# Bias bands from the host, and dense tiles dealt over the jobs of attention and the samples' compressed branch

## The chip, the cores and the metric

One core of one Trainium2 chip. The metric is the device time of one execution in microseconds. Float32 data throughout; large matmuls take fp32r operands split into a high and a low part.

## The reference, cut to what matters

One layer of a hybrid decoder for a prompt of 512 rows and 8 samples of one row each with 1024 cached rows. h = x(1 + scale) + shift goes through one wide input projection. Two mixers run on its parts: native sparse attention (8 heads on 2 groups of keys: a compressed, a selected and a window branch, gated) and MoBA (8 heads, blocks of 256). Every logit gets a T5 bias by distance. Then gates, two up projections, a merge by sigmoid gates, an output projection, a residual and a layer norm.

```python
parts = jnp.split(h @ w_in, np.cumsum(IN_WIDTHS)[:-1], axis=-1)
(a_q, a_kc, a_vc, a_ks, a_vs, a_kw, a_vw, a_g, a_z, b_q, b_k, b_v, b_z, m_a, m_b) = parts
# each branch: softmax(q . k / 8 + bias[bucket(distance)]) v
y_a = (o_a * silu(a_z)) @ w_up_a
y_b = (o_b * silu(b_z)) @ w_up_b
mixed = (sigmoid(m_a) * y_a + sigmoid(m_b) * y_b) @ w_out
x_new = layer_norm(ALPHA * x + gate * mixed, ln_g, ln_b)
```

For the prompt all blocks are selected, so both mixers are causal attention there. The samples read their caches (cmp, slc, moba: 64 pages of 128 rows) and select blocks.

## The kernel before, in words

**Dense tiles.** The input projection is cut into tiles of 128 output channels, named in FILLS: q, z, bq, bz, bk, bv, vs, vw, kw, and m0 to m7, each of which is two tiles, ma and mb. `dense` makes a tile with 48 matmuls (8 steps of depth, 3 products of high and low parts, 2 halves of 260 columns) in 4 units of 12. Its weights come through the feed W: one load of 512 KB on SP's queue into a ring of 4 raw tiles, a copy on ACT (L310) and a subtraction on POOL or DVE (L231) into the split hl. W follows one fixed list, SEQ. K and V tiles are also written out (`evac`, ok); m tiles made while attention runs go to DRAM and back (m_d).

**Order.** The program is written by generators that `merge` interleaves: of several flows the one that has done the smallest share of its total goes next. Totals are written by hand (PHIS, ATT, DEC, and 5328 for a dense tile). A scheduler then fixes the order on each engine when the kernel is compiled: by its own estimate of times it issues the ready instruction that stands first in the program. `issue_after` and `order` add an edge of issue order on one engine, without a wait for completion; `high_priority` puts an instruction ahead of the rest of the program. On the chip each engine and SP's queue run strictly in that order.

**Stages.** (1) Start: adaLN, the tiles kc, vc, ks, and the bias tables (`tables`). (2) FILLS[0] merged with `phis`, which compresses the cached rows of the samples. At its end POOL's queue sends the band bs (16 heads x 384 biases, repeated for 128 rows) into the DRAM tile band_d, L939. (3) `dec_cmp`: the compressed branch of the samples, written into the program alone (drain, L942). (4) Attention of the prompt, `attend` for 8 pairs of heads: pairs 0 to 3 with 4 jobs, pairs 4 to 7 with 2. `prepare` loads the pair's band from band_d by a shifted view (L960) and splits q. A job scores 4 row tiles (`score`: 2 matmuls into one of 2 PSUM banks s, a minimum with the band on DVE at L1011, exp on ACT at L1015, scaling on POOL at L1017), turns p with 10 transposes (L1024), and every second job `value` multiplies by V; the pipe is three jobs deep. Each pair is merged with FILLS[pi + 1] and with a part of `dec`, up to DEC_SHARE[pi] of DEC. (5) `dec` is the samples' attention over the feed C: loads of 1 MB into 2 buffers, of which slck takes 16 issues on SP each, mobk and mobv 4, and slcv two gathers on POOL's queue. (6) FILLS[9] merged with the rest of `dec`. (7) up and output projections and the norm.

SP's queue issues the weight loads, the cache loads, the bands and the stores, one behind the other.

## Time and profile before

| | us |
|---|---|
| Median of 3 runs | 657.74 (655.98 to 663.47) |
| Profiled execution, its own time | 656.24 |
| Span of its trace, first to last instruction | 654.5 |
| TensorE (PE) busy | 610.4 |
| VectorE (DVE) busy | 311.0 |
| ScalarE (ACT) busy | 294.9 |
| GpSimd (POOL) busy | 288.5 |
| Mean granted TensorE clock, share of full speed | 0.984 |

Times in the trace count from the span's start. Attention's exps run from 184.7 to 489.3; the up projections begin at 541. TensorE's matmuls are pipelined, so a busy TensorE is not one at its peak.

### The profile page before, as it was taken

Reading aid. Unit: us, or ns where it says so; the run is one execution under the profiler, and the core shown is the slowest. Engines: PE = TensorE matmul, PEld = TensorE weight load, DVE = VectorE, ACT = ScalarE, POOL = GpSimd, SP = SyncE. Lnnn points to the kernel's source line nnn. Section 1 sums busy time; section 2 is a strip of 40 time slices with the busy share of each in tenths; the row PEclk is TensorE's granted clock in tenths of the full one; section 3 lists DMA queues with packets and bytes.
Section 4 is the critical chain, followed back from the end, with each engine's and each line's share of the span. In section 5 each row is a group of like instructions: output and inputs, shape, how many; then the busy total and the mean of one; then the engine's idle time right before and its main releaser. Section 6 shows DMA issues by size and latency. Waiting matters only on the chain.

```text
span 654.5 us, 13320 instructions
## 1 busy us (share of the span) xinstructions
PE 610.4 (93%) x4747; PEld 509.7 (78%) x4747; DVE 311.0 (48%) x800; ACT 294.9 (45%) x679; POOL 288.5 (44%) x328
## 2 busy tenths in 40 slices
PE   5999999999979699999999899998987999999993
PEld 4779999999968378776879679866635998999672
DVE  1465545433563663334355447735431155545177
ACT  2247556434444445534445447635333353432521
POOL 1105586551442323433364545535332264655646
PEclk9999999999999979999999999999999999999997
DMA  8995565539943683798875562269887353345202
GB/s 305 355 292 187 169 193 171 170 76 109 200 140 103 203 334 109 251 312 290 262 252 157 209 226 91 62 224 325 295 265 280 97 166 126 97 130 180 78 28 104
DMA packets 64132, 124.77 MB, mean 191 GB/s; under 512 B 8142, under 2 KB 28368, under 8 KB 63521
## 3 DMA queue, kind: packets, MB, share of 16 engines
q1 hardware_dynamic: 61954, 116.58, 53.6%
q0 software_dynamic: 2112, 7.34, 6.3%
q8 instruction: 37, 0.61, 0.4%
q14 instruction: 29, 0.24, 0.1%
HBM read 112.76 MB, written 11.13 MB: 189 GB/s over the span
## 4 chain that ended last, share of the span: by engine, by line
PE 57%; DMA 12%; SPq 5%; DVE 3%; issue 2%; POOL 1%; ACT 1%; POOLq 0%; ACTq 0%; DVEq 0%
PE d L199 33%; PE s L199 8%; PE e L199 6%; DMA band_d<-bs 6%; SPq L721 4%; DMA raw<-mobv 4%; PE pt L1024 3%; PE o L202 2%; PE o L199 2%; PE pt L199 1%; PE e L202 1%; DMA ew<-tabx 1%; DMA raw<-slcv,vidx 1%; DMA raw<-winv 1%; SPq L717 1%
## 5 line engine op out<-in xcount | busy, mean ns | idle before, releaser
L199 PE MATMUL d<-hTh,hl 128*128 128x260 f32 (+1 forms) x1408 | 269.4, 288 | 1.6 <-DVE hl L231 1.1
L199 PEld LDWEIGHTS d<-hTh,hl 128*128 128x128 f32 (+1 forms) x1408 | 218.6, 187 | 15.8 <-issue 9.4
L199 PE MATMUL d<-hTl,hl 128*128 128x260 f32 (+1 forms) x704 | 199.5, 284 | 0.0
L199 PEld LDWEIGHTS d<-hTl,hl 128*128 128x128 f32 (+1 forms) x704 | 131.6, 187 | 3.1 <-issue 2.5
L231 POOL TENSOR_TENSOR hl<-raw,hl 128x512 fp32r<-128x512 f32 x56 | 74.0, 1321 | 101.6 <-ACT hl L310 97.0
L310 ACT CAST hl<-raw 128x512 fp32r<-128x512 f32 (+1 forms) x111 | 67.8, 615 | 75.5 <-PE d L199 63.0
L1017 POOL TENSOR_SCALAR p<-p,sm,gp 128x512 f32<-128x512 f32 (+1 forms) x64 | 39.9, 623 | 95.9 <-DVE sm L1016 91.3
L1015 ACT ACTIVATE p<-s,sm 128x512 f32<-128x512 f32 (+1 forms) x96 | 50.8, 529 | 66.9 <-PE pt L1024 52.2
L231 DVE TENSOR_TENSOR hl<-raw,hl 128x512 fp32r<-128x512 f32 (+1 forms) x55 | 53.5, 974 | 49.1 <-ACT hl L310 47.3
L199 PE MATMUL d<-yh,hl 128*128 128x260 f32 x256 | 46.3, 282 | 0.0
L1024 PE MATMUL pt<-cst,p 128*128 128x128 f32 x240 | 40.6, 283 | 1.5 <-DVE pp L1029 0.8
L199 PEld LDWEIGHTS d<-yh,hl 128*128 128x128 f32 x256 | 39.8, 188 | 1.0 <-issue 0.4
L199 PE MATMUL s<-kd,q 128*128 128x512 f32 (+1 forms) x96 | 35.2, 367 | 4.6 <-ACT p L1015 4.6
L1009 DVE TENSOR_REDUCE sm<-s 128x1 f32<-128x256 f32 (+1 forms) x48 | 16.9, 354 | 42.7 <-PE s L199 41.7
L1024 PEld LDWEIGHTS pt<-cst,p 128*128 128x128 f32 x240 | 28.0, 143 | 11.6 <-issue 5.9
L199 PE MATMUL d<-yl,hl 128*128 128x260 f32 x128 | 36.0, 282 | 0.0
L1017 POOL TENSOR_SCALAR p<-p,sm,cst 128x512 f32<-128x512 f32 (+3 forms) x32 | 19.5, 608 | 37.2 <-DVE sm L1016 36.8
L1011 DVE CUSTOM_DVE_ANT_0 s<-s,band 128x256 f32<-128x256 f32 (+1 forms) x48 | 17.3, 362 | 36.8 <-PE s L199 23.6
L199 PEld LDWEIGHTS s<-kd,q 128*128 128x128 f32 x96 | 18.4, 191 | 18.3 <-ACT p L1015 7.7
L199 PE MATMUL s<-u,w1h 128*128 128x256 f32 (+1 forms) x160 | 30.1, 283 | 2.1 <-ACT u L827 0.8
L199 PE MATMUL s<-kd,qx 128*128 128x512 f32 (+1 forms) x96 | 31.5, 331 | 0.0
L231 POOL TENSOR_TENSOR u<-craw,u 128x512 fp32r<-128x512 f32 x16 | 22.0, 1377 | 21.6 <-ACT u L827 21.6
(425 smaller groups left out, 1158.3 us busy)
## 6 DMA issues: line engine op xcount, KB each, us to landing
raw<-w_cols SPq DMA_DIRECT2D x46, 512.0 KB
raw<-mobk SPq DMA_DIRECT2D x64, 256.0 KB
raw<-mobv SPq DMA_DIRECT2D x64, 256.0 KB
u<-ada_ss SPq DMA_DIRECT2D x16, 512.0 KB
craw<-cmp SPq DMA_DIRECT2D x64, 128.0 KB
raw<-slck SPq DMA_DIRECT2D x64, 64.0 KB
raw<-ada_g SPq DMA_DIRECT2D x8, 512.0 KB
raw<-w_up SPq DMA_DIRECT2D x8, 512.0 KB
```

What stands on the lines that cost most here:

```text
L199: i = mmraw(out, lhsT, rhs, start=start, stop=stop, skip_group_check=True)
L202: i = mmraw(out, lhsT, rhs, start=start, stop=stop, skip_group_check=True)
L231: (nc.gpsimd if eng == "p" else nc.vector).tensor_sub(out, x, f32(hi))
L310: nc.scalar.copy(h, src)
L717: _, pages = nc.values_load_multi_w_load_instructions(ptt[0:1, k0:k0 + step * (len(outs) - 1) + 1:step], engines=(mybir.EngineType.SP,), m ...
L721: dyn.append(nc.sync.dma_start(out, A[name][bass.ds(page, 1)].rearrange("a p c -> p (a c)")))
L1009: nc.vector.tensor_reduce(sm[:, 0:1], s[:, :b], axis=AX, op=OP.min)
L1011: nc.vector.tensor_tensor_reduce(out=s[:, b:n], in0=s[:, b:n], in1=j.band[:, 256 - (n - b):], scale=1.0, scalar=top, op0=OP.add, op1=OP.mi ...
L1015: nc.scalar.activation(pr, s[:, :n], AF.Exp, scale=-1.0, bias=sm[:, 1:2], accum_out=sm[:, 2:3])
L1017: nc.gpsimd.tensor_scalar(pr, pr, sm[:, 3:4], j.gate(i), op0=OP.mult, op1=OP.mult)
L1024: nc.tensor.transpose(p[:, k * 128:k * 128 + 128], j.p[i][:, kb * 128:kb * 128 + 128], ident)
```

## The change

The bias bands are computed on the host, one [128, 2, 256] tile for each pair (input `band`); the device keeps the last bias of each head in every partition (blast) and turns the loaded band into blast - band with two POOL instructions. band_d, bs, its matmul, its copy and its write are gone. The tiles bq2, bq0 and bq3 are merged with `dec_cmp` (CMP_FILLS); the other lists are dealt anew, ATT and DEC_SHARE too. The first matmul of every unit of a dense tile stands in issue order behind the 12th last score of the program (`hold`); the matmuls of `dec_cmp` stand behind the dense matmul written last (`behind`). From attention on, weight loads and the stores of ok and m_d have high priority (W.first).

```diff
+FILLS = [["ks", "vs", "ag", "vw", "q0", "kw", "q1", "q2", "q3"],
+         ["bq1", "m0", "m1"],
+         ["bv0", "bk0", "m2"],
+         ["z0", "bv1", "m3"],
+         ["z1", "bv2", "m4"],
+         ["bk1", "z2"],
+         ["bk2", "bv3", "bk3"],
+         ["z3", "bz0"],
+         ["bz1", "m5"],
+         ["bz2", "m6", "g0", "g1", "bz3", "g2", "g3", "m7"]]
+CMP_FILLS = ["bq2", "bq0", "bq3"]
-DEC_SHARE = [0.09, 0.15, 0.28, 0.31, 0.37, 0.45, 0.52, 0.66]
+DEC_SHARE = [0.13, 0.26, 0.39, 0.5, 0.57, 0.64, 0.78, 0.92]
-ATT = [20400, 20000, 17000, 47040, 10800, 5250, 7500, 9000]
+ATT = [17100] * 4 + [7100] * 3 + [11000]
+AHEAD = 12
-BAND_AT = 3
...
+    scored, dense_mm = [], []
+
+    def hold(i):
+
+        if len(scored) >= AHEAD:
+            order(i, scored[-AHEAD])
+
+    def behind(i):
+
+        order(i, dense_mm[-1])
+        return i
...
-                    if self.after is None:
+                    if self.first:
+                        with tc.high_priority():
+                            fn(t[:, :n])
+                    elif self.after is None:
...
-            p = p_e()
-            mm(p[:16, :384], tabx[:, 0:16], e[:, E_BAND:E_CMP], True, True)
-            bs = st.tile([16, 384], F32, name="bs")
-            nc.vector.tensor_copy(bs, p[:16, :384])
-            D["band"] = bs
...
+            nc.sync.dma_start(blast, bass.AP(tensor=A["tabx"].tensor, offset=A["tabx"].offset + 31 * 272, ap=[[0, 128], [1, 16]]))
...
-                            mm(acc[bk][:M, :HB], hl[:, x, kk * M:kk * M + M], hb[:, k, bk * HB:bk * HB + HB],
-                               k == 0 and j == 0, k == 7 and j == 2)
+                            i = mm(acc[bk][:M, :HB], hl[:, x, kk * M:kk * M + M], hb[:, k, bk * HB:bk * HB + HB],
+                                   k == 0 and j == 0, k == 7 and j == 2)
+                            if kk == 0 and j == 0:
+                                hold(i)
+                            dense_mm[:] = [i]
...
-            nc.sync.dma_start(A["ok"][KOUT.index(name)], ev)
+            with tc.high_priority() if W.first else ExitStack():
+                nc.sync.dma_start(A["ok"][KOUT.index(name)], ev)
...
-                    nc.sync.dma_start(m_d[c][:, i], to)
+                    with tc.high_priority():
+                        nc.sync.dma_start(m_d[c][:, i], to)
...
+            yield 5
             p = p_e()
             with together():
                 for b in range(NS):
-                    mm(p[grp(b % 4), :64], zn[:, b], ckd[:, b], b < 4, b >= 4)
-            yield 700
+                    i = mm(p[grp(b % 4), :64], zn[:, b], ckd[:, b], b < 4, b >= 4)
+                    if b == 0:
+                        behind(i)
+            yield 2
...
-            mm(p[:, :64], const("gsum"), xc, True, True)
+            behind(mm(p[:, :64], const("gsum"), xc, True, True))
+            yield 1
...
-                if bp == BAND_AT:
-                    with tc.issue_after(D["last"].ins):
-                        nc.gpsimd.dma_start(band_d[:, :, 0:384], D["band"].unsqueeze(1).to_broadcast([16, 128, 384]))
...
-        drain(dec_cmp())
+
+        merge(Flow(fills(CMP_FILLS), fill_cost(CMP_FILLS)), Flow(dec_cmp(), 12.0))
...
+        W.first = True
...
-            nc.sync.dma_start(bt, bass.AP(tensor=band_d.tensor, offset=band_d.offset + h0 * 128 * 385 + 127,
-                                          ap=[[384, 128], [hs * 128 * 385, 2], [1, 256]]))
+            nc.sync.dma_start(bt, A["band"][pi])
+            for g in range(2):
+                h = h0 + g * hs
+                nc.gpsimd.tensor_scalar(bt[:, g], bt[:, g], blast[:, h:h + 1], -1.0, op0=OP.subtract, op1=OP.mult)
...
-                mm(s[:, :n], j.q2[k][:, i * 128:i * 128 + 128], j.kd[:, :n], k == 0, k == 1)
+                m = mm(s[:, :n], j.q2[k][:, i * 128:i * 128 + 128], j.kd[:, :n], k == 0, k == 1)
+            scored.append(m)
...
+    dist = 128 + np.arange(128)[:, None] - np.arange(256)[None]
+    heads = [[p, p + 4] if p < 4 else [2 * p, 2 * p + 1] for p in range(8)]
+    band = np.where((dist < 0)[..., None], np.float32(-BIG), inp["rel_bias"][_bucket(dist)])
+    d["band"] = f(np.stack([band[:, :, h].transpose(0, 2, 1) for h in heads]))
```

The lists of before, and the program order they give, are in the functions printed above: FILLS[0] had bq2 besides, the pairs 2, 2, 4, 5, 3, 4, 3 and 1, and FILLS[9] 11 with the four gate loads between them.

## Rows read from the trace of the kernel before

**Rows 1.** The page: busy us, share of the span and instructions of each engine.
```profile
PE 610.4 (93%) x4747; PEld 509.7 (78%) x4747; DVE 311.0 (48%) x800; ACT 294.9 (45%) x679; POOL 288.5 (44%) x328
```

**Rows 2.** Windows by stage: stretch, length, busy of five engines (x), clock, DMA share, GB/s.
```profile
142.00:179.00 37.00, 36.82 (x310) 36.32 (x309) 13.83 (x38) 15.71 (x33) 13.44 (x15) 1.00 0.93 135
179.00:240.00 61.00, 49.97 (x336) 38.68 (x335) 34.37 (x98) 25.77 (x67) 22.05 (x27) 0.92 0.60 200
240.00:360.00 120.00, 120.00 (x985) 95.30 (x983) 54.64 (x185) 59.00 (x152) 50.26 (x60) 1.00 0.70 231
360.00:440.00 80.00, 76.14 (x667) 62.18 (x666) 44.30 (x133) 43.58 (x114) 37.82 (x46) 0.98 0.48 161
440.00:500.00 60.00, 51.53 (x378) 29.84 (x377) 22.53 (x82) 25.74 (x70) 23.52 (x30) 1.00 0.88 302
541.00:641.00 100.00, 100.00 (x653) 85.34 (x652) 51.58 (x94) 36.62 (x60) 56.33 (x56) 1.00 0.32 104
```

**Rows 3.** Waits of PE over the span: us in total, times, longest.
```profile
PE e L199 <- DMA raw<-mobv: 6.1, 8, 1.4
PE e L199 <- DMA raw<-slck: 5.3, 4, 3.4
PE s L199 <- ACT p L1015: 5.3, 9, 1.4
PE e L199 <- DMA ew<-tabx: 2.5, 1, 2.5
```

**Rows 4.** Windows, dense matmuls on hTl alone: length, PE busy (x), clock, DMA share, GB/s.
```profile
179.00:211.00 32.00, 15.12 (x53) 1.00 0.44 131
211.00:234.00 23.00, 0.01 (x1) 0.86 0.71 240
179.00:489.00 310.00, 104.20 (x365) 0.98 0.65 216
440.00:500.00 60.00, 9.03 (x32) 1.00 0.88 302
500.00:541.00 41.00, 29.18 (x104) 1.00 0.45 146
```

**Rows 5.** Timeline of SP's queue, 160 to 240: start, us, line, transfer.
```profile
165.39 0.33 SPq L342 DMA_DIRECT2D raw<-w_cols  x1
166.72 3.01 SPq L572 DMA_DIRECT2D ok<-ev  x1
179.00 0.90 SPq L960 DMA_DIRECT2D band<-band_d  x2
180.43 40.45 SPq L721 DMA_DIRECT2D raw<-slck  x64
...
223.21 0.42 SPq L342 DMA_DIRECT2D raw<-w_cols  x1
```

**Rows 6.** The tile band_d: its write, issued at 142.5, to its landing.
```profile
DMA to landing us min/median/max: 36.4/36.4/36.4
```

**Rows 7.** Timeline of SP's queue, 440 to 500.
```profile
474.98 10.94 SPq L721 DMA_DIRECT2D raw<-mobv  x12
...
489.67 0.91 SPq L342 DMA_DIRECT2D raw<-w_cols  x2
```

**Rows 8.** Groups of instructions by form on POOL: busy, mean ns, idle before.
```profile
L1017 POOL TENSOR_SCALAR p<-p,sm,gp 128x256 f32<-128x256 f32 x16 | 8.9, 554 | 16.5 <-DVE sm L1016 14.1 <-PE d L199 2.2
```

**Rows 9.** The chain that ended last, 498 to 566: start, us, what.
```profile
500.39 26.04 PE d L199 x216
```

**Rows 10.** The line of the exps: duration ns, first and last start, forms.
```profile
L1015 ACT ACTIVATE p<-s,sm x96: 361/527/722, 184.7 to 489.3; 128x512 f32<-128x512 f32 x24, 128x384 f32<-128x384 f32 x24, 128x256 f32<-128x256 f32 x24, 128x128 f32<-128x128 f32 x24
```

**Rows 11.** Windows of that line alone: length, ACT busy (x), clock, DMA share, GB/s.
```profile
210.50:221.50 11.00, 2.76 (x9) 1.00 0.37 102
```

**Rows 12.** Timeline of PE, 155 to 161, without its dense matmuls.
```profile
155.85 0.31 PE L202 MATMUL e<-ckd,zn 128*32 128x64 f32 x4
...
160.51 0.33 PE L199 MATMUL e<-xc,cstd 128*128 128x64 f32 x2
```

More of the change, by code (lines that the diff above doesn't have):

```diff
@@ L35 @@
         + [f"{n}{c}" for c in range(8) for n in ("ma", "mb")])
-FILLS = [["ks", "vs", "ag", "vw", "q0", "bq2", "kw", "q1", "q2", "q3"],
-         ["bq0", "bq1"],
-         ["bq3", "bv0"],
-         ["z0", "bk0", "m0"],
-         ["bv1", "z1", "m1", "bv2"],
-         ["bk1", "m2"],
-         ["z2", "bk2", "m3"],
-         ["bv3", "z3", "bk3"],
-         ["bz0"],
-         ["bz1", "bz3", "bz2", "g0", "m4", "g1", "g2", "m5", "m6", "g3", "m7"]]
-DEC_SHARE = [0.09, 0.15, 0.28, 0.31, 0.37, 0.45, 0.52, 0.66]
+FILLS = [["ks", "vs", "ag", "vw", "q0", "kw", "q1", "q2", "q3"],
[10 more added lines that the diff above has]
+DEC_SHARE = [0.13, 0.26, 0.39, 0.5, 0.57, 0.64, 0.78, 0.92]
 DEC, DEC_PACE = 50000.0, 0.875
 PHIS = 49353.58399999998
-ATT = [20400, 20000, 17000, 47040, 10800, 5250, 7500, 9000]
+ATT = [17100] * 4 + [7100] * 3 + [11000]
+AHEAD = 12
 SECOND = [3, 4, 6, 7]
@@ L62 @@
 SEQ = (COLS[:3]
-       + [n for f in FILLS for i in f if i != "ks" for n in ([f"ma{i[1]}", f"mb{i[1]}"] if i[0] == "m" else
+       + [n for f in (FILLS[0], CMP_FILLS, *FILLS[1:]) for i in f if i != "ks" for n in ([f"ma{i[1]}", f"mb{i[1]}"] if i[0] == "m" else
                                           [f"g{2 * int(i[1])}", f"g{2 * int(i[1]) + 1}"] if i[0] == "g" else [i])]
@@ L283, in __init__ @@
                 self.after = None
+                self.first = False
             def load_to(self, i):
@@ L375, in build @@
         ocmp = per.tile([128, 128], F32, name="ocmp")
+        blast = per.tile([128, 16], F32, name="blast")
         m_d = dram.tile([8, 128, 2, NT], F32, name="m_d")
-        band_d = dram.tile([16, 128, 385], F32, name="band_d")
         y = yp.tile([128, 8, NT], F32, name="y", tag="y")
@@ L910, in dec_cmp @@
             p = p_e()
-            nc.tensor.transpose(p[:64, :128], xc, ident)
+            behind(nc.tensor.transpose(p[:64, :128], xc, ident))
+            yield 1
             zc = f32(u_tile())[:, 0, :512].rearrange("p (a b) -> p a b", a=4)
@@ L916, in dec_cmp @@
                                       view(p[:64], b2 * 32, [[8, 2], [64, 2], [1, 8]]))
-            yield 200
             p = p_e()
             for bp in range(4):
-                mm(p[:, :128], zc[:, bp], cvd[:, bp], bp == 0, bp == 3)
+                i = mm(p[:, :128], zc[:, bp], cvd[:, bp], bp == 0, bp == 3)
+                if bp == 0:
+                    behind(i)
             nc.vector.tensor_copy(ocmp, p[:, :128])
+            yield 1
             for c in range(2):
                 new_scores(c, pp)
-            yield 500
+            yield 1
         W.after = ss["dma"]
```

## The prediction

> **What bounds the kernel now.** First the page: TensorE is busy 610.4 us, 93% of the span, every other compute engine under half [rows 1]. So TensorE's work, in its order, sets the time, and a change that leaves that work alone can win only where TensorE stands still. The windows by stage say where [rows 2]. It is full in 142 to 179 (36.82 of 37), in 240 to 360 and from 541 to 641. It stands still in 179 to 240 (49.97 of 61: 11.0 idle; and a mean granted clock of 0.92, a part of it at the lower level of 1.2 GHz, costs 8% of 61, 4.9 more), in 360 to 440 (3.9 idle, 2% of 80 or 1.6 by the clock) and in 440 to 500 (8.5 idle). That is 15.9 + 5.5 + 8.5 = 29.9 us of room. The profiled execution took 656.24 us, so the floor for any rearrangement of this part is near 626.
>
> Next, what TensorE waits for [rows 3]: loads of the cache (mobv 6.1, slck 5.3) and, for 5.3, a score whose PSUM bank the softmax still holds; 2.5 go to ew, the window's bias. These name what came last, not why nothing else stood in the queue. The count of one dense matmul form, a third of a tile's 48, shows that [rows 4]. There are 53 in 179 to 211 (3.3 tiles) and 1 in 211 to 234: the dense tiles ran ahead of the scores until none was left. In 440 to 500 there are 32 (2 tiles); in 500 to 541, behind attention, where nothing is left to hide, 104 (6.5 tiles).
>
> Why none was left stands on SP's queue [rows 5]. A weight load goes out at 165.39, the next at 223.21. Between them SP stands from 169.7 to 179.00, 9.3 us, before the first band load, then spends 40.45 us on issuing the 64 small slck loads, and the weights are behind these. DMA itself was not full: 0.44 in 179 to 211 [rows 4]. The 179.00 comes from the band, 3 MB that POOL's queue sends into DRAM in 36.4 us [rows 6]. In 440 to 500 the pattern returns: twelve mobv issues stand on SP before two weight loads at 489.67 [rows 7].
>
> **The change part by part.** *Band.* Gone: one matmul and one copy at the start (under waits for loads there), the 36.4 us write and the load's wait for it. The eight band loads stay, now of an input. Added: a 64-byte row to each partition early on, and two POOL passes of 128x256 for each of 8 pairs. The like POOL scaling takes 554 ns [rows 8]: 16 x 0.55 = 8.9 us on an engine that is 44% busy [rows 1]. If nothing covers them, each pair's softmax waits 1.1 us, 9 us in all; seven tiles of p lie between POOL and the transposes, so I take 0. SP reaches the slck loads up to 9.3 us sooner, and of TensorE's 5.3 us for slck the longest wait, 3.4, goes.
>
> *Weights first* (W.first): the weight loads, with the stores of ok and m_d, no longer queue behind cache loads. This refills 211 to 234. The other side: if SP comes to a weight load whose ring slot is still being split, it stands, and the slck, mobk and mobv loads behind it stand too, and so do TensorE's decode matmuls. Bounds: nothing, to one wait like the 9.3 [rows 5] for a pair. I take 1 us in all, nearer to nothing, since SP's 40 us for slck fit into a first pair of some 50.
>
> *Tiles dealt out, and hold.* The pairs get 5, 4, 4, 4, 2, 3, 2 and 3 tiles (27), 3 go beside dec_cmp, and 6 stay for the end, near the 6.5 that run there now. A tile costs 48 x 26.04 / 216 = 5.8 us [rows 9]; their number is the same, so this part is worth only the gaps it fills. A unit may be at most 12 scores, three jobs, ahead; the price comes if the chain of scores is slower than TensorE, for then the held units wait behind it. From the first exp to the last, 184.7 to 489.3, 96 scores go at 3.2 us each [rows 10], idle time and all; where no dense tile was in front (210.5 to 221.5), 9 ACT instructions, two to a score, make 2.4 us each [rows 11]. TensorE's own need in the new order I reckon so: busy from 179 to the last exp 50 + 120 + 76 + 49/60 of 51.5 = 288 [rows 2], less 6.5 by the clock and 4 for loads and gates dealt elsewhere, plus some 2.2 tiles (13 us): 27 less about 2 that can run ahead of the first score, against 365 / 16 = 22.8 in 179 to 489 now [rows 4]. That is 290, or 3.0 a score. 2.4 is under 3.0, so the hold should not bite: I take 0, and keep the other end as a rival.
>
> *dec_cmp under three tiles.* Its matmuls keep a place behind the dense unit before them. In the old order the longest step, scores to group sums, is 155.85 to 160.51, 4.7 us [rows 12], and two units of 1.46 us are dealt into it: 1.7 might stay bare. Four such steps make 0 to 6 us; free units of pair 0 can fill them, so I take 1.
>
> *m4 and m5* go through m_d as m0 to m3 do: 1 MB more written and read, 2.1 MB at the 302 GB/s of rows 2, 7 us of DMA. Dense work covers it; without that cover it would be 7, and I take 0.
>
> *The last two pairs* now hold 13 of 16 mobv items and 5 tiles. Bytes: 13 x 1.05 MB, 5 x 0.52 MB and about 0.8 of stores and bands, 17 MB, at the 302 GB/s of 440 to 500 57 us. TensorE: 51.5 busy there less 2 tiles (11.6) is 40 for 4.6 jobs and 16 items, so about 34 for 4 jobs and 13 items, and 29 for 5 tiles: 63 us. The loads fit under it, narrowly, so I count half of the 8.5 as won.
>
> The sum: of 15.9 in 179 to 240, ew's 2.5 and the other slck waits (1.9) stay: 11.5 won. Of 5.5 in 360 to 440, where gathers with two buffers stay as they are, half: 2.7. Of 8.5, half: 4.2. Less 1 for SP and 1 for dec_cmp: 16.4. 656.24 - 16.4 = 639.8. The median of the runs shown, 657.74, is 1.5 above the profiled one; with half of that on top: 641.
>
> **A rule against it.** SP has 64 issues in 40.45 us for 4 MB, with DMA 0.44 busy [rows 4, 5]. The Trainium skill (DMA: Bandwidth & Descriptors, Issuing engines are not separate DMA queues) says that the sequencer's time to initiate a DMA is usually small relative to the DMA itself. By that rule the weights were late by transfers, their place in the queue would give nothing, and of the 11.5 only the band's 3.4 would be won: 648 instead of 641. The row disagrees for loads this small. The Trainium skill's Perfetto Trace Analysis, What "DMA-bound" means, names the case that the row shows: the issuing engine's track is solid with DMA slices.
>
> **The rivals.** (a) *All the room is filled*: 626 to 633. For it, 240 to 360 runs the same mixture without a gap at a DMA share of 0.70 [rows 2]; against it, ew and the gathers are not touched. 0.12. (b) *The queue's order is only turned round*: weights go out in time, cache loads late, and TensorE stands before decode matmuls instead of before dense ones. Won: the band's 3.4; the 4.2 of the last pairs and the rest come back as waits for slck and mobv: 651 to 660, about 654. For it: two buffers for cache loads, 0.88 of DMA in 440 to 500 [rows 2]; against it: 0.44 in 179 to 211. 0.18. (c) *Slower, by the hold*: the scores set the pace. From the last exp to the first up matmul stay 52 us, from there to the end 113.5, outside the span 1.7; with the first exp 10 us sooner, at 174.7, the time is 342 + 95 x pace: at 3.0 627, at 3.15 641, at 3.4 665, at 3.5 674. It decides from 3.4 on, and would give about 672. For it: the 3.2 of now; against it: the 2.4 without dense work in front [rows 10, 11]. 0.14. (d) the forecast, 633 to 651: 0.56.
>
> **The numbers.** A measurement of this kernel can tell about 1% from no change: under 651.2 is faster, over 664.3 slower. Faster is (a) and (d), 0.68; same is (b), 0.18; slower is (c), 0.14. The range of 8 in 10 runs from the floor, 626, to 660, the end of (b); (d) alone has 633 to 651.
>
> **What would show it.** Right: no 23 us without dense matmuls; the longest stretch between two weight loads on SP far under the 58 us of now; TensorE's idle time from 179 to 500, now 23 us, under 10; the first exp some 10 us sooner; a granted clock near 1.00 where it was 0.92; the stretch behind the last exp as long as now. Wrong: waits of TensorE for slck or mobv of over 10 us each (b); over 3.3 us between exps with TensorE waiting for the softmax (c); or a gap in dec_cmp of more than 3 us.

## The result

The changed kernel takes 663.16 us (median of 20 runs, 659.65 to 670.67), the kernel before 657.39 us beside it (20 runs). The ratio is 1.0091, 95% interval 1.0069 to 1.0114: 0.9% slower, 22 us above the forecast of 641 and 3 us above its range. The profiled execution took 664.92 us with a span of 663.2. The experiments' times, ratios and means below leave out executions over 1.5% above the same kernel's fastest, two of them at 1227 and 2107 us, while a median that an expectation quotes has them in.

The page of the changed kernel; first the busy time, share and instructions of each engine, as [rows 1] of before:

```profile
PE 616.0 (93%) x4745; PEld 514.8 (78%) x4745; DVE 312.7 (47%) x799; ACT 294.9 (44%) x679; POOL 305.4 (46%) x343
```

The windows by stage, as [rows 2] (stretch, length, busy of PE, PEld, DVE, ACT, POOL with counts, granted clock, DMA share, GB/s):

```profile
142.00:179.00 37.00, 33.22 (x277) 32.27 (x276) 14.31 (x38) 14.70 (x32) 15.89 (x17) 0.97 0.31 99
179.00:240.00 61.00, 59.30 (x444) 50.53 (x444) 34.02 (x103) 32.50 (x83) 28.25 (x32) 0.96 0.64 206
240.00:360.00 120.00, 112.49 (x922) 86.61 (x924) 50.93 (x180) 52.24 (x137) 55.40 (x63) 0.99 0.68 229
360.00:440.00 80.00, 73.21 (x617) 63.59 (x618) 44.47 (x125) 43.74 (x111) 39.75 (x46) 0.98 0.33 110
440.00:500.00 60.00, 58.26 (x447) 42.16 (x445) 25.17 (x83) 27.35 (x74) 25.74 (x33) 1.00 0.81 276
500.00:541.00 41.00, 37.74 (x273) 24.82 (x270) 9.64 (x19) 12.56 (x29) 11.80 (x15) 0.92 0.76 260
541.00:641.00 100.00, 100.00 (x662) 86.68 (x662) 48.85 (x80) 39.57 (x65) 56.17 (x57) 1.00 0.34 111
```

Beside [rows 2] the two holes are closed: 179 to 240 stands still for 1.7 us instead of 11.0, 440 to 500 for 1.7 instead of 8.5. The time came back elsewhere. 142 to 179, full before, stands for 3.8; 240 to 360, full before, for 7.5; 360 to 440 for 6.8 instead of 3.9; 500 to 541 for 3.3, at a clock of 0.92. The kernel before was full in this last stretch too:

```profile
500.00:541.00 41.00, 41.00 (x343) 39.71 (x340) 12.88 (x13) 16.73 (x34) 15.64 (x14) 1.00 0.45 146
```

From 142 to 541 TensorE stands for 24.8 us in all, against 23.5 before.

The longest waits of PE over the span, as [rows 3]:

```profile
PE s L200 <- ACT p L1044: 8.0, 12, 2.1
PE e L200 <- DMA y<-e: 6.4, 1, 6.4
PE s L200 <- DVE q L997: 3.6, 2, 2.5
PE e L200 <- DMA raw<-mobv: 2.8, 3, 1.8
PE d L200 <- DVE hTh L469: 2.6, 1, 2.6
PE e L200 <- DMA raw<-mobk: 2.5, 4, 1.1
PE e L200 <- DMA raw<-winv: 1.7, 1, 1.7
PE pt L1053 <- POOL p L1046: 1.7, 2, 1.5
PE e L200 <- DMA raw<-slck: 1.7, 2, 1.4
```

The waits for slck and mobv fell from 11.4 us to 4.5, and ew's is gone. Part of that came back at other cache loads: 4.2 us for mobk and winv, where the kernel before has 0.7 for winv and none for mobk. The wait of a score for the softmax (L1044, L1015 before) grew from 5.3 to 8.0. Those for q and hTh are new; the one for y was there before, with 6.6.

SP's queue is in the order that was meant, against [rows 5] (start, us, line, transfer):

```profile
169.86 0.80 SPq L986 DMA_DIRECT2D band<-band  x2
171.22 3.80 SPq L740 DMA_DIRECT2D raw<-slck  x7
...
189.25 0.37 SPq L359 DMA_DIRECT2D raw<-w_cols  x1
...
202.90 0.37 SPq L359 DMA_DIRECT2D raw<-w_cols  x1
```

The first band is loaded at 169.86 instead of 179.00, and the weights stand between the slck loads.

### The profile page after: what moved, and what is told of

It reads as the page before. It is cut to its first block, busy times and chain, and to the rows that moved or that the text cites. A ratio compares the mean times of both kernels' runs of the same rounds, so it can differ in the third digit from the quotient of the medians.

```text
span 663.2 us, 13356 instructions
## 1 busy us (share of the span) xinstructions
PE 616.0 (93%) x4745; PEld 514.8 (78%) x4745; DVE 312.7 (47%) x799; ACT 294.9 (44%) x679; POOL 305.4 (46%) x343
## 4 chain that ended last, share of the span: by engine, by line
PE 69%; DMA 10%; DVE 5%; SPq 5%; ACT 4%; issue 4%; POOL 2%; POOLq 0%; ACTq 0%; DVEq 0%
PE d L200 39%; PE s L200 11%; PE e L200 7%; SPq L740 4%; DMA raw<-mobk 4%; PE o L200 3%; PE o L203 2%; PE pt L1053 2%; DMA raw<-mobv 2%; DMA craw<-cmp 2%; PE pt L200 2%; PE e L203 1%; ACT u L846 1%; ACT p L1044 1%; DVE u L244 1%
## 5 line engine op out<-in xcount | busy, mean ns | idle before, releaser
L200 PE MATMUL d<-hTh,hl 128*128 128x260 f32 (+1 forms) x1408 | 274.5, 290 | 1.1 <-DVE vnew L616 0.8
L200 PEld LDWEIGHTS d<-hTh,hl 128*128 128x128 f32 (+1 forms) x1408 | 223.5, 190 | 15.1 <-issue 10.9
L200 PE MATMUL d<-hTl,hl 128*128 128x260 f32 (+1 forms) x704 | 202.2, 289 | 0.0
L200 PEld LDWEIGHTS d<-hTl,hl 128*128 128x128 f32 (+1 forms) x704 | 133.5, 190 | 6.2 <-issue 5.9
L1044 ACT ACTIVATE p<-s,sm 128x512 f32<-128x512 f32 (+1 forms) x96 | 50.9, 530 | 65.7 <-PE pt L1053 46.1
L1038 DVE TENSOR_REDUCE sm<-s 128x1 f32<-128x256 f32 (+1 forms) x48 | 17.0, 355 | 44.5 <-PE s L200 33.1
L1046 POOL TENSOR_SCALAR p<-p,sm,cst 128x512 f32<-128x512 f32 (+3 forms) x32 | 20.1, 627 | 34.3 <-DVE sm L1045 26.8
L999 POOL TENSOR_TENSOR qx<-y,q 64x512 fp32r<-64x512 f32 x16 | 24.9, 1559 | 13.7 <-ACT q L996 7.3
```

The lines of the kernel that those rows point to most:

```text
L200: i = mmraw(out, lhsT, rhs, start=start, stop=stop, skip_group_check=True)
L999: nc.gpsimd.tensor_sub(qx[own], y[own, pi, :T], f32(q2[own]))
L1038: nc.vector.tensor_reduce(sm[:, 0:1], s[:, :b], axis=AX, op=OP.min)
L1044: nc.scalar.activation(pr, s[:, :n], AF.Exp, scale=-1.0, bias=sm[:, 1:2], accum_out=sm[:, 2:3])
L1046: nc.gpsimd.tensor_scalar(pr, pr, sm[:, 3:4], j.gate(i), op0=OP.mult, op1=OP.mult)
```

## The experiments

Each kernel is compared with the kernel before, measured beside it; us is the median. For every kernel I give two more means over its executions, from the span and the mean granted clock that each lists: *clock* is span x (1 - granted clock), and *rest* is span x granted clock, which holds TensorE's work and its waits. *clock* is the most that the lower level of TensorE's clock can have cost: where TensorE stands at that level, nothing is lost by it.

| kernel | us | ratio to before (95%) | clock | rest |
|---|---|---|---|---|
| before (five times) | 656.7 to 659.3 | 1 | 14.8 to 16.8 | 640.0 to 640.5 |
| changed | 663.1 | 1.0091 (1.0069 to 1.0114) | 15.2 | 646.5 |
| a_nohold | 662.3 | 1.0092 (1.0056 to 1.0128) | 20.7 | 640.6 |
| a_nowfirst | 664.6 | 1.0134 (1.0083 to 1.0184) | 16.0 | 646.9 |
| a_start | 672.8 | 1.0239 (1.0185 to 1.0293) | 20.8 | 649.9 |
| a_start_swap | 667.1 | 1.0136 (1.0077 to 1.0194) | 20.1 | 645.6 |
| a_keep | 662.3 | 1.0112 (1.0048 to 1.0175) | 15.7 | 645.4 |
| a_oldshare | 662.0 | 1.0064 (1.0023 to 1.0106) | 17.8 | 642.5 |
| a_oldshare_nohold | 651.6 | 0.9921 (0.9878 to 0.9964) | 12.2 | 638.5 |
| b_band | 661.3 | 1.0069 (1.0039 to 1.0100) | 12.5 | 646.8 |
| b_band_start | 663.4 | 1.0088 (1.0053 to 1.0124) | 12.3 | 648.8 |
| b_band_keep | 654.7 | 0.9937 (0.9905 to 0.9969) | 10.4 | 643.1 |
| b_wfirst | 656.7 | 1.0032 (0.9992 to 1.0071) | 14.5 | 640.9 |
| c_band_w_start | 654.1 | 0.9947 (0.9907 to 0.9988) | 10.0 | 642.4 |
| c_keep | 651.0 | 0.9897 (0.9849 to 0.9945) | 9.1 | 640.4 |
| c_cmp | 651.7 | 0.9899 (0.9868 to 0.9929) | 11.0 | 639.0 |
| c_cmp_hold | 670.3 | 1.0165 (1.0129 to 1.0201) | 21.3 | 647.4 |
| c_lists | 654.4 | 0.9922 (0.9884 to 0.9959) | 13.2 | 639.3 |
| c_lists_share | 671.7 | 1.0224 (1.0168 to 1.0281) | 26.8 | 643.6 |
| c_deal | 670.9 | 1.0217 (1.0162 to 1.0272) | 27.0 | 643.1 |

Names with a_ start from the changed kernel, those with b_ and c_ from the kernel before; c_ has the bands and the weights first. Against the kernel before, the changed one is level in *clock* and 6 us higher in *rest*.

### One part undone, one part alone

Three theories stood at the start: the hold costs the time (H), the queue's order is only turned round (Q), and time is lost at the start (S).

**a_nohold**: the changed kernel without the hold.

```diff
-AHEAD = 12
+AHEAD = 10 ** 9
```

> The changed kernel with AHEAD so large that no dense unit is held behind a score. Theory H (the hold leaves TensorE without ready work where it waits for a score's bank or a cache load): the 8.7 us lost in 240 to 360 and the 8.4 in 360 to 440 come down to the few us of the kernel before, dense units run ahead again, and the time is 648 to 655. Rival Q (weights sent first make the cache loads late): the waits for mobk, winv and mobv stay, the time stays at 661 to 666. Rival S (the loss lies in the start, 3 to 4 us, and behind the last score): the time also stays, 660 to 666, and the first adaLN matmul still starts at 11.6.

Measured 662.3, as with the hold. In this kernel the hold is neutral in the sum, but not in its parts: without it the rest is 5.9 us less and the clock's loss 5.5 us more. That is taken up below.

**a_nowfirst**: the changed kernel, weight loads and stores back in their old place.

```diff
-        W.first = True
+        W.first = False
```

> The changed kernel without the high priority of weight loads and of the ok stores (W.first False). Theory Q: waits for mobk, winv and slck fall, but the weights queue behind the slck issues again, so a stretch of 40 us or more without a weight load on SP and 10 us lost in 179 to 240: 660 to 670. Theory H: the held units hide that the weights are late less well than before, 665 to 675. If weights first was worth what the prediction says (8 us), it is 668 to 674.

Measured 664.6; the interval overlaps that of the changed kernel. Weights first cost nothing that can be told, so Q falls as the cause of the slowdown.

**b_band**: the kernel before with the host's bands alone (input, blast, two POOL passes; band_d, its write, its matmul and its copy gone).

```diff
-                    with tc.issue_after(D["last"].ins):
-                        nc.gpsimd.dma_start(band_d[:, :, 0:384], ...)
...
+            nc.sync.dma_start(bt, A["band"][pi])
+            for g in range(2):
+                h = h0 + g * hs
+                nc.gpsimd.tensor_scalar(bt[:, g], bt[:, g], blast[:, h:h + 1], -1.0, op0=OP.subtract, op1=OP.mult)
```

> The kernel before with the bands from the host alone. Theory S: without the band's matmul and its copy in the one PSUM bank e, the table matmuls stand ahead of the first adaLN matmul, which starts near 11.6 instead of 7.9, and the first phi matmul near 61 instead of 57.4: 3 to 4 us lost; against that the wait of SP for the band's write (9.3 us) is gone, and 0 to 5 us of that are won: 656 to 661. If the start is not the band's doing, 652 to 656.

Measured 661.3: alone, this part makes the kernel slower than before. In its trace the first adaLN matmul goes out 3.9 us later than in b_band_keep (below), which has the band's matmul. The timeline of PE in b_band, then the same in b_band_keep (start, us, line, out<-in, form):

```profile
6.37 5.26 PE L198 MATMUL e<-y 33*128 33x8 f32 x24 [6.37 <-DMA y<-e]
11.55 1.08 PE L198 MATMUL s<-u,cs 128*32 128x256 f32 x8
```

```profile
6.24 1.44 PE L198 MATMUL e<-y 33*16 33x384 f32 x2 [6.24 <-DMA y<-e]
7.61 1.08 PE L198 MATMUL s<-u,cs 128*32 128x256 f32 x8
8.62 4.43 PE L198 MATMUL e<-y 33*128 33x8 f32 x20
```

With the band's matmul and copy gone, the scheduler puts all 24 table matmuls ahead of adaLN's first. That it is their PSUM bank which held the table matmuls back, as expected above, no run shows apart from the matmul and the copy.

**b_wfirst**: the kernel before with the weights and stores first, alone.

```diff
+                    if self.first:
+                        with tc.high_priority():
+                            fn(t[:, :n])
...
+        W.first = True
```

> The kernel before with the high priority of weight loads and stores alone. The prediction: the 23 us without dense matmuls after 211 are filled and 5 to 10 us are won: 648 to 653. Theory Q: the cache loads come later by what the weights come sooner, 655 to 662, with waits for slck or mobv of over 8 us.

Measured 656.7, no change that can be told. Yet the hole is filled:

```profile
179.00:240.00 61.00, 56.64 (x412) 47.73 (x413) 33.55 (x95) 30.27 (x77) 21.91 (x27) 0.94 0.70 217
```

TensorE is busy for 56.64 us of a stretch in which it was busy for 49.97 [rows 2] (in the profiled execution, the fastest of this kernel's: 652.8), and over the runs the kernel is not faster. This is the first sign that a filled hole need not be a gain.

### The start

**a_start**: the changed kernel, with the table matmuls queued behind the second adaLN unit's first matmul.

```diff
-                tables()
+                with tc.issue_after(D["seli"].ins):
+                    tables()
```

> The changed kernel, with one edit: the table matmuls of the start are queued behind the first matmul of the second adaLN unit, so that they no longer stand in front of the first adaLN matmul, which in all kernels without the band's own matmul went out at 11.6 us instead of 7.9. Theory S (a good part of the slowdown is lost at the start, by the band's matmul being gone): first adaLN matmul back near 7.9, TensorE's idle time up to the compressed branch down from 9.2 to about 7, and 3 to 4 us less in all, 659 to 660. Theory R (a gain ahead is spent again at later waits, whose order is set by the loads and the softmax): the start comes back, and the total stays within 1 us of 663.

Measured 672.8, a miss. The first adaLN matmul goes out at 7.4, but the next ones then wait for their loads:

```profile
PE s L200 <- DMA u<-ada_ss: 8.4, 3, 7.4
```

The table matmuls had covered that wait. The edit only moved the stall, so it doesn't test S. It is 9.7 us over the changed kernel (by the means 5.6 in *clock* and 3.4 in *rest*); where they come from isn't settled.

**b_band_start**: the same edit of `tables()` on b_band.

> The kernel before with the bands from the host alone, and the same edit of the start. The bands alone gave 661.3. Theory S: the bands cost nothing of their own, and with the start mended it is 656 to 657.5, no slower than before. Theory P (the POOL passes over the bands, or the later first exp, cost the time): it stays at 660 to 661 with the start mended.

Measured 663.4, no better than b_band, for the same reason. P was not ruled out by this run.

**c_band_w_start**: the kernel before with bands, weights first and that start; no new dealing, no hold.

> The kernel before with the bands, the weight loads ahead of the cache loads and the edit of the start, but with the old dealing of tiles, no hold, and the compressed branch's softmax bare: everything of the change but the dealing. If the dealing of tiles is what eats the gain (theory D), this is faster than the changed kernel with the same start by 4 us or more, 652 to 655. If the dealing is worth what it was meant for, it is slower than that one by 2 us or more. Theory R says that the two lie within 2 us of each other.

Measured 654.1: 18.7 us under a_start, which differs by the dealing (the tiles beside the compressed branch among it) and the hold. D holds, far beyond its 4 us, for all of these together.

**a_start_swap**: a_start with the gate tiles m0 and m1 dealt to later pairs.

```diff
-         ["bq1", "m0", "m1"],
-         ["bv0", "bk0", "m2"],
+         ["bq1", "bv0", "bk0", "m0"],
+         ["m1", "m2"],
```

> The changed kernel with the edit of the start, and the two gate tiles m0 and m1 dealt to later pairs (m0 behind the rank tiles of the first pair, m1 and m2 to the second). In the changed kernel ma0 holds two PSUM banks from 169 to 175 us because its output tile lives in a pool that opens only behind the compressed branch, and TensorE is idle for 3.8 us in 142 to 179. If that is the cause of the loss at attention's opening, idle time in 142 to 179 falls by 3 us or more, and the total is 3 to 5 us under the same kernel without this edit; if what ends attention is set by later waits, idle time falls there and the total stays within 1 us.

Measured 667.1, 5.7 under a_start, with intervals that overlap slightly. The expected cause is not borne out: in 142 to 179 TensorE still stands for 3.3 us, against 3.8 in a_start. So where the difference comes from, if it is one, isn't shown.

**c_keep**: the kernel before with bands and weights first; the band's matmul and copy are left in, with nobody to read them, so that the start is issued as before.

```diff
+            mm(p[:16, :384], tabx[:, 0:16], e[:, E_BAND:E_CMP], True, True)
+            bs = st.tile([16, 384], F32, name="bs")
+            nc.vector.tensor_copy(bs, p[:16, :384])
```

> The kernel before with the host's bands and the weight loads ahead of the cache loads, the old dealing, no hold and the compressed branch bare; and the band's matmul and its DVE copy at the start are left in, their result unused, so that the start is issued in the order of the kernel before. Theory S: all kernels without that matmul lose 2 to 4 us up to the compressed branch's first matmul (58.5 to 64.3 against 57.4 us), so here that point is at 57 to 58 us, and the time is 3 to 6 us under the one with the other edit of the start (656.5), 650 to 653: faster than before by 0.6 to 1.1%. If the start's loss is of the loads, the point stays at 60 or over, and the time at 656 to 658.

Measured 651.0, the fastest of all: 1.0% under the kernel before and, by the two ratios (0.9897 / 1.0091), 1.9% under the changed one. The first matmul of `phis`, which the expectation calls the compressed branch's first, is at 56.9 us (57.4 before, 61.6 in the changed kernel). S holds here.

**b_band_keep**: the bands alone, with the band's matmul left in. (Run later, put here as it belongs to S.)

> The kernel before with the bands from the host alone, and the band's matmul and copy left in at the start. Bands alone without that matmul gave 661.3. Theory S: 3 to 5 us less, 656 to 658, level with the kernel before; then the bands give nothing without the order of the weights, and the weights nothing without the bands (658.0), but both together 651. If it stays at 661, the bands cost something of their own, and the order of the weights is worth 10 us on top of them.

Measured 654.7, against 661.3 without the matmul; the intervals don't meet. So the bands alone are worth 0.6%, and the lost place of that matmul cost them 1.3%. My expectation had them level with before.

**a_keep**: the changed kernel with the matmul left in.

> The changed kernel with the same matmul and copy left in at the start and nothing else changed. Theory S: 658 to 660, 3 to 5 us under 663. Theory D (the new dealing of tiles costs time): this stays above the kernel with the old dealing and the same start by 6 us or more.

Measured 662.3, from four executions: no gain that can be told, though the trace starts as before (56.9). In the changed kernel the 4.7 us won at the start are lost again before the end; S explains the bands, not the whole. It lies 11.3 us above c_keep: D again.

### The dealing, taken apart

**c_cmp**: c_keep with bq2, bq0 and bq3 beside the compressed branch, the other tiles in their old order.

```diff
-        drain(dec_cmp())
+        merge(Flow(fills(CMP_FILLS), fill_cost(CMP_FILLS)), Flow(dec_cmp(), 12.0))
...
-         ["bq0", "bq1"],
-         ["bq3", "bv0"],
-         ["z0", "bk0", "m0"],
+         ["bq1", "bv0"],
+         ["z0", "bk0"],
+         ["m0"],
```

> The kernel c_keep plus one part of the dealing: bq2, bq0 and bq3 merged with the compressed branch, its matmuls behind the dense unit written last; the other tiles keep their old order, dealt to the pairs as before except that the first three take bq1, bv0, then z0, bk0, then m0. If this part carries the cost of the dealing (theory D1), it is slower than c_keep by 4 us or more; if the new lists for the pairs carry it (D2), it lies within 2 us of c_keep.

Measured 651.7: with the old lists this part costs nothing.

**c_deal**: c_keep with the new lists, shares and totals of the pairs; no hold, the compressed branch bare.

```diff
+         ["bq0", "bq3", "bq1", "m0", "m1"],
+         ["bv0", "bk0", "m2"],
+         ["z0", "bv1", "m3"],
...
+DEC_SHARE = [0.13, 0.26, 0.39, 0.5, 0.57, 0.64, 0.78, 0.92]
+ATT = [17100] * 4 + [7100] * 3 + [11000]
```

> The kernel c_keep plus the other part of the dealing: the new lists, shares and totals for the pairs (27 tiles and 0.92 of the samples' attention inside the pairs, gate tiles first), with no hold and the compressed branch bare; bq2 stays in the first list, bq0 and bq3 open the first pair's. Theory D2: slower than c_keep by 5 us or more, with the loss between the first and the last score. D1: within 2 us of c_keep.

Measured 670.9, 19.9 above c_keep: D2. Of this the rest has 2.7 and the clock 17.9 (27.0 against 9.1).

**c_lists**: c_deal without the last two lines of its diff, that is c_keep with the new lists alone.

> The kernel c_keep plus the new lists of tiles for the pairs (27 tiles inside the pairs, gate tiles first) with the old shares of the samples' attention and the old totals. Theory L (the lists carry the cost of the dealing: four more tiles inside attention stretch it by more than they take from the end): 665 to 671. Theory P (the shares carry it: 0.92 instead of 0.66 of the samples' attention inside the pairs): 650 to 654. Both together: 657 to 662.

Measured 654.4, within the noise of c_keep. The lists aren't it.

**c_lists_share**: c_lists with the new shares of the samples' attention, the totals still the old ones.

```diff
-DEC_SHARE = [0.09, 0.15, 0.28, 0.31, 0.37, 0.45, 0.52, 0.66]
+DEC_SHARE = [0.13, 0.26, 0.39, 0.5, 0.57, 0.64, 0.78, 0.92]
```

> The kernel c_lists (new lists, no hold, the compressed branch bare) with the new shares of the samples' attention, and the totals as they were. c_lists gave 654.6, the same with shares and totals 670.9. If the shares carry it (0.92 of the samples' attention inside the pairs, so that its cache loads and scores crowd the softmax's stretch): 667 to 672. If the totals carry it (how one pair's scores, tiles and cache items are mixed): 653 to 658.

Measured 671.7, 17.3 above c_lists and level with c_deal: the shares alone carry it. The windows of the two show where. First the page's line and the windows of c_lists:

```profile
PE 610.8 (94%) x4747; PEld 511.3 (78%) x4747; DVE 309.2 (47%) x800; ACT 294.3 (45%) x679; POOL 308.2 (47%) x343
260.00:353.00 93.00, 92.73 (x735) 76.16 (x733) 36.64 (x122) 44.07 (x115) 40.05 (x47) 1.00 0.66 221
353.00:420.00 67.00, 61.99 (x613) 50.92 (x611) 39.65 (x129) 34.83 (x94) 39.63 (x46) 1.00 0.61 206
486.00:520.00 34.00, 26.63 (x173) 13.45 (x173) 6.49 (x25) 10.40 (x29) 7.28 (x10) 0.90 0.83 286
```

Then c_lists_share:

```profile
PE 623.4 (93%) x4747; PEld 519.7 (78%) x4747; DVE 307.1 (46%) x800; ACT 294.9 (44%) x679; POOL 306.4 (46%) x343
260.00:360.00 100.00, 94.99 (x837) 73.94 (x839) 39.84 (x128) 42.12 (x110) 45.12 (x51) 0.98 0.81 271
360.00:420.00 60.00, 54.86 (x430) 48.15 (x423) 32.17 (x106) 30.43 (x82) 26.34 (x33) 0.91 0.32 106
498.00:532.00 34.00, 26.91 (x123) 13.15 (x122) 9.09 (x35) 13.57 (x37) 9.88 (x16) 0.70 0.41 140
498.00:514.40 16.40, 14.86 (x58) 8.71 (x57) 5.84 (x25) 7.03 (x21) 4.77 (x8) 0.58 0.08 30
```

With the new shares the cache items are used up early. 260 to 360 is dense with them (DMA 0.81, 271 GB/s), and TensorE stands for 5.0 us there where c_lists stands for 0.3. 360 to 420 has few left (0.32, 106 GB/s): TensorE stands for 5.1 us there, as in c_lists (5.0), but at a clock of 0.91 where c_lists has 1.00. From 499 to the last score at 514.4 neither an item nor a tile runs, and the last eight scores go bare: from 498 on TensorE stands for 1.5 us only, but its clock is 0.58. One matmul of a score there, from the timeline of PE (start, us, line, out<-in, form, and what it waited for):

```profile
507.66 0.69 PE L198 MATMUL s<-kd,q 128*128 128x384 f32 x1 [0.34 <-ACT p L1021]
```

c_lists stands just as long in its own last stretch (7.4 of 34 us, against 7.1), 3.1 of it for mobv loads; but its clock is 0.90 there and 0.70 here. Over the whole of the two profiled executions the same 4747 matmuls keep TensorE busy for 623.4 us instead of 610.8, while it stands for 44.5 instead of 42.3. Over all executions the shares cost 13.6 us in *clock* and 4.3 in *rest*.

**c_cmp_hold**: c_cmp with the hold.

```diff
+                            if kk == 0 and j == 0:
+                                hold(i)
```

> The kernel c_cmp plus the hold: the whole change except the new lists, shares and totals of the pairs, with the band's matmul left in at the start. Tiles run ahead of their pairs by about four pairs' worth without the hold. If the hold has a price of its own when few tiles are dealt to a pair (theory H: TensorE then stands for the softmax, scores' pace 3.2 us), 657 to 662. If it is neutral, as it was in the changed kernel (662.6 without, 663.2 with it), within 2 us of c_cmp, 650 to 654.

Measured 670.3, 18.6 above c_cmp: H, after all, at 8 us over the range that was expected for it. With the old lists few tiles are dealt to the first pairs, and the hold keeps back those of the later ones. The stretch of the first 48 scores, in c_cmp and then in c_cmp_hold, with the longest wait of PE in the latter:

```profile
175.00:349.00 174.00, 168.34 (x1291) 135.22 (x1290) 82.64 (x259) 83.61 (x212) 76.55 (x90) 0.99 0.68 220
```

```profile
163.00:304.00 141.00, 123.12 (x835) 84.97 (x835) 74.51 (x244) 66.25 (x174) 62.59 (x72) 0.93 0.60 195
PE s L200 <- ACT p L1045: 9.0, 17, 2.4
```

The scores go faster, 2.9 us each (141 / 48) instead of 3.6, but TensorE stands for 17.9 us, half of it for the softmax, and its clock falls to 0.93. Only 6.5 dense tiles run there, against 15.75 in c_cmp; the others run behind.

**a_oldshare**: the changed kernel, band's matmul left in, with the old shares and totals.

```diff
-DEC_SHARE = [0.13, 0.26, 0.39, 0.5, 0.57, 0.64, 0.78, 0.92]
-ATT = [17100] * 4 + [7100] * 3 + [11000]
+DEC_SHARE = [0.09, 0.15, 0.28, 0.31, 0.37, 0.45, 0.52, 0.66]
+ATT = [20400, 20000, 17000, 47040, 10800, 5250, 7500, 9000]
```

> The whole changed kernel, the band's matmul left in at the start, with the old shares of the samples' attention (0.66 inside the pairs) and the old totals. Theory P (shares and totals cost some 16 us): 665.4 falls to 650 to 655. If P held only where there is no hold: it stays at 662 to 668. Theory H (the hold has a price of its own as soon as the shares don't hide it, as with the old lists): 660 to 670, and the next one 10 us or more under it.

Measured 662.0, level with a_keep (662.3). P doesn't hold while the hold is on.

**a_oldshare_nohold**: the same with AHEAD = 10 ** 9, without the hold.

> The same without the hold: bands, weights first, tiles beside the compressed branch and the new lists, with old shares and totals. It differs from c_lists (654.6) by the tiles beside the compressed branch alone, which cost nothing with the old lists, so 652 to 657. Theory H: 10 us or more under the one with the hold; theory P: within 3 us of it.

Measured 651.6, 10.4 under the one with the hold: H holds with the new lists too, once the shares are the old ones.

So the hold costs 18.6 with the old lists, 10.4 with the new ones, and nothing that can be told with the new lists and shares; the shares cost 17.3 without the hold, and with it nothing that can be told. The 17.3 was measured with the compressed branch bare. a_nohold and c_deal, both with the new lists and shares and no hold, differ by the tiles beside that branch and by the band's matmul, and a_nohold is 8.6 us faster; it is 10.7 over a_oldshare_nohold, which has the old shares (and the band's matmul). So in the changed kernel's own setting the price of the shares is nearer to 11, like that of the hold. The two aren't additive, and the counts fit this reason: the hold keeps tiles for the end that the shares strip of cache items. The first 48 scores of the changed kernel have 13.5 tiles among them and the others 13.5; without the hold it is 15.9 and 11.1. No run holds back the tiles of one end alone. The stretch from 488 to 515, the last scores, in the changed kernel and then in a_nohold:

```profile
488.00:515.00 27.00, 26.81 (x208) 17.75 (x206) 8.07 (x30) 7.78 (x23) 6.77 (x10) 1.00 0.87 284
```

```profile
488.00:515.00 27.00, 20.65 (x116) 12.15 (x112) 9.04 (x38) 10.25 (x30) 9.77 (x17) 0.76 0.38 132
```

With the hold, TensorE is full there at full clock, with the units of bz2 and m6 and cache items among the scores; without it it stands for 6.4 us at a clock of 0.76. By these windows each of the two settings takes the cover from one end of attention, the hold from the first pairs, the shares from the last.

## Why the prediction was wrong, point by point

Two steps failed. The sum took 16.4 us as won, where the best that bands and weights first gave is 6.8 (c_keep). And the dealing, priced at nothing but what it fills, costs some 11 us on top: with the hold, with the new shares or with both the kernel takes 662 to 663, and without either 651.6 (a_oldshare_nohold).

*The holes* (right). Weights first, and a band that waits for nothing, closed 179 to 240, and the waits for slck and mobv fell. The longest stretch between two weight loads in attention's first half is 20.1 us, from 169.1; in the second, one of 58.1 us from 454.1 stands where [rows 7] had its like, with gate loads in it; by the sign that I had named, far under 58, that part failed. The clock in 179 to 240 is 0.96, not 1.00, and from 179 to 500 TensorE stands for 17.7 us, not under 10.

*The sum* (the first step that failed). I took the idle time of each stretch as won where its wait went, and the full stretches as staying full. The tiles that fill a hole are taken from a later place. The count of dense matmuls on hTl (16 to a tile) between the first and the 49th score, and from there to the last, in the kernel before:

```profile
177.40:347.00 169.60, 61.88 (x216) 40.97 (x215) 0.00 (x0) 0.97 0.68 228
347.00:485.80 138.80, 43.07 (x152) 28.59 (x152) 0.00 (x0) 0.99 0.61 202
```

and in c_keep, which has bands and weights first and nothing else:

```profile
172.80:344.80 172.00, 72.27 (x252) 48.09 (x252) 0.00 (x0) 0.99 0.69 223
344.80:475.70 130.90, 35.39 (x124) 23.38 (x124) 0.00 (x0) 1.00 0.59 199
```

The first half does 2.25 tiles more, the second 1.75 fewer. The windows over the same two stretches and the one from the last score to the up projections, with all matmuls, show what that did to TensorE, in the kernel before and then in c_keep:

```profile
177.40:347.00 169.60, 158.57 (x1179) 123.44 (x1177) 82.66 (x257) 79.76 (x206) 69.05 (x82) 0.97 0.68 228
347.00:485.80 138.80, 130.69 (x1120) 100.28 (x1119) 73.38 (x237) 70.30 (x187) 62.38 (x78) 0.99 0.61 202
485.80:541.00 55.20, 50.98 (x417) 43.55 (x414) 14.26 (x18) 21.87 (x48) 19.38 (x19) 1.00 0.58 194
```

```profile
172.80:344.80 172.00, 167.94 (x1288) 134.85 (x1287) 82.60 (x259) 83.60 (x212) 76.05 (x90) 0.99 0.69 223
344.80:475.70 130.90, 119.60 (x1029) 89.08 (x1027) 71.41 (x235) 67.36 (x180) 70.53 (x84) 1.00 0.59 199
475.70:535.50 59.80, 53.78 (x425) 44.02 (x422) 13.74 (x18) 21.77 (x48) 19.98 (x19) 0.97 0.55 185
```

It stands for 4.1, 11.3 and 6.0 us in c_keep, where the kernel before stands for 11.0, 8.1 and 4.2: of the 7.0 won in the first half 5.0 are lost behind it. Over all executions the *rest* of c_keep is that of before (640.4 against 640.2); its gain is in *clock*, 9.1 us instead of 15.0, which I had put beside the idle time as the smaller share. How the 6.8 us split is less sure than these means say: between the two profiled executions TensorE is busy for 2.4 us less and stands for 3.3 less.

*The band* (right in sign, wrong in what it takes along). It is worth 0.6% by itself. The POOL passes take 1.14 us each where I took 0.55:

```profile
L989 POOL TENSOR_SCALAR band<-band,blast x16: 1127/1144/1987, 176.7 to 459.8; 128x256 f32<-128x256 f32 x16
```

They are covered: PE waits for POOL's p for 1.7 us in all. I priced the removed matmul at nothing, as a thing under waits for loads. It decided what the scheduler put ahead of adaLN; without it the bands alone are 1.3% slower.

*Weights first* (right, smaller). On top of the bands they give 3.7 us (654.7 to 651.0; the intervals overlap, so it may be nothing), alone nothing. If they do need each other, SP's queue has a reason: with the weights alone the band load still waits until 178.12; with the bands alone SP still issues 64 slck loads in 40.48 us ahead of the weights.

*The hold* (wrong, the second step that failed). I took 0, as 2.4 us a score is under TensorE's 3.0. The 2.4 was read in 11 us, off five exps. Over 48 scores with 6.5 tiles beside them the pace is 2.9 (c_cmp_hold), about the 3.0 that I reckoned as TensorE's need: no slack is left for the hold. The hold costs 18.6 us with the old lists and 10.4 with the new lists and the old shares. Rival (c) had the mechanism and the place, and its 672 is about what the hold gives with the old lists (670.3). In the changed kernel it doesn't decide alone: without it the time is the same, as the new shares then cost as much. Its pace there:

```profile
L1044 ACT ACTIVATE p<-s,sm x96: 357/528/714, 182.7 to 513.3; 128x512 f32<-128x512 f32 x24, 128x384 f32<-128x384 f32 x24, 128x256 f32<-128x256 f32 x24, 128x128 f32<-128x128 f32 x24
```

That is 3.5 us from exp to exp, over (c)'s bound of 3.4, with 8.0 us of waits for the softmax, so (c)'s sign of being wrong came; and the first exp is 2 us sooner than in [rows 10], not 10. By (c)'s formula the time would be 680; it is 665 since the stretch from the last exp to the up projections shrank with its tiles, from 52 us to 37.

*The shares* (the term that is missing). I weighed the last two pairs by bytes and TensorE time, 57 against 63 us, and found that they fit. They did: 440 to 500 went from 8.5 us idle to 1.7. What I didn't ask is what is left for the scores behind, and in 360 to 440. Where there is no hold they cost 17.3 us with the compressed branch bare, most of it in *clock*, and some 11 in the changed kernel's setting; that is rival (c)'s size from another mechanism.

*dec_cmp* (right). c_cmp costs nothing against c_keep; I took 1. With the new lists and shares it may even be worth something (a_nohold against c_deal). *m4 and m5* and the new lists as a whole: 654.4 against 651.0, within the noise, I took 0.

*Rival (b)*, no gain since the order is only turned round, ends 3 us under the measured time (651 to 660), but its waits for slck and mobv shrank; rival (c), slower by the hold, begins 2 us above it (665 at a pace of 3.4). What stays open: why the start won back in a_keep brings nothing there, and where a_start's 9.7 us over the changed kernel come from.

I had also weighed the Trainium skill's sentence that a sequencer's time to initiate a DMA is usually small beside the DMA itself (DMA: Bandwidth & Descriptors, Issuing engines are not separate DMA queues), and concluded from it that the weights' place in the queue would give nothing. This case's traces don't agree with the sentence for these loads: in b_band_keep too SP takes 40.48 us for 64 issues, where 4.2 MB at the 302 GB/s of [rows 2] would be some 14, an estimate. And in b_wfirst order alone fills the hole. Yet on the gain in time that conclusion came nearer than my sum, for another reason: the filler was missing later. (Its 648 stands before the half of 1.5 us that the 641 has on top; with it, it is 649.)

## What to carry to other kernels

In this kernel an idle stretch on the bounding engine was worth something only where the work that filled it didn't leave a stretch elsewhere: count the filler (tiles, cache items) for every stretch before and after, and look for who runs bare last. The scores here, short steps that wait for each other, needed cover to the last one, so a filler that was dealt out early, or held back, moved the hole to the other end. Two settings that each cost time can hide each other's price: undo both before calling one neutral. And leave a dead instruction's place in the order in mind: taking it away can reorder what stood behind it.

## What the hardware showed that was not expected

Where the scores lost their cover, the granted clock carried as much of the difference as TensorE's waits, or more: 13.6 of 17.9 us between c_lists and c_lists_share, 10.3 of 18.7 between c_cmp and c_cmp_hold, as the means *clock* and *rest* have it. (Between the kernel before and the changed one it carried next to none.) Long stands aren't needed for that: the bare scores of c_lists_share stand for 1.5 of 16.4 us, at a clock of 0.58. In the changed kernel the first score at 174.11 and the compressed scores behind it wait for q, and TensorE does most of the next unit at half its clock, 1.2 instead of 2.4 GHz; two matmuls of the same form take 0.40 us ahead of the stand and 0.64 behind it (timeline, then the window of that stretch):

```profile
171.97 0.40 PE L200 MATMUL d<-hTh,hl 128*128 128x260 f32 x2
...
177.16 1.70 PE L200 MATMUL s<-ck,q 128*128 128x64 f32 x7 [2.52 <-DVE q L997]
...
179.25 0.64 PE L200 MATMUL d<-hTh,hl 128*128 128x260 f32 x2
```

```profile
177.00:183.00 6.00, 5.84 (x25) 5.75 (x26) 4.40 (x14) 1.27 (x3) 5.91 (x6) 0.50 0.42 128
```

So here a stand of 2.5 us was followed by 6 us at half the clock: on the bounding engine it cost more than its length.
